# A state space layer computed in chunks of four tokens, inside a two-block network on one core

## The chip, the cores and the metric

The kernel runs on one core of one Trainium2 chip. The metric is device time in microseconds (us). TensorE (PE) multiplies matrices, VectorE (DVE), ScalarE (ACT) and GpSimd (POOL) do the rest, and DMA queues are fed by SyncE (SP) and by ScalarE's own instruction stream.

## The reference, cut to what matters

Two transformer blocks over 256 tokens of width 2048, all in float32. The part that changes is the state space layer ("SSM") of the second block: 64 groups of 16 channels, each with 64 complex states, so 32 tiles of 128 states for 8 tiles of 128 channels.

```python
    abar_re = mag * jnp.cos(li * dt)
    abar_im = mag * jnp.sin(li * dt)
    ...
    bu_re = jnp.einsum('blgh,gph->lbgp', ug, bbar_re)
    bu_im = jnp.einsum('blgh,gph->lbgp', ug, bbar_im)
    ...
    _, _, s_re, s_im = lax.associative_scan(_ssm_combine, (a_re, a_im, bu_re, bu_im), axis=0)
    y = (jnp.einsum('lbgp,ghp->blgh', s_re, c_re.astype(jnp.float32))
         - jnp.einsum('lbgp,ghp->blgh', s_im, c_im.astype(jnp.float32))
         + d_skip.astype(jnp.float32).reshape(SSM_GROUPS, SSM_GROUP) * ug)
    y = jax.nn.gelu(y.reshape(bsz, seq, SSM_WIDTH)).astype(u.dtype)
    return y * jax.nn.sigmoid(y @ w_glu + b_glu)
```

The matrices `abar`, `bbar` and `c` come from inputs, so they are worked out on the chip too.

## The kernel before

Six stages follow one another, named here as in the table below: pool, mlp0, attn, mlp1, mix2 (the SSM and the latent attention side by side), ffn. Activations lie transposed, features on the partitions and 256 tokens along the row. Weights stream once through the core: SP issues loads of 1 MB into three raw buffers; ACT makes the high part of each unit of 128x1024 numbers (`hi`, L145) and DVE the low part (`lo`, L153), three units ahead of PE (two for `lo` in mix2), with five buffers of each. PE then does the 16 to 24 matmuls of the unit (L203 to L211). That is one "tick" of some 2.8 us. After a tick the host code steps every live generator (the evacuation of a finished sum, in pieces) and runs one entry of a background list. So the program order of each engine, fixed when the kernel is built, is weight work with other work let in between.

The SSM appears in three places. `ssm_params` (pool stage, background, one step a tick) computes magnitudes, angles and the input and output matrices on DVE (L892 and others), turns them with 32 PE transposes (L948, L949) and writes them to DRAM (`d_q`). `tables` (mlp0, background, on POOL: L985, L991, L1005) doubles a table exp(i theta t) of every state up to 256 tokens and writes it to DRAM (`d_tab`, L1009). In mix2, `ssm_step` runs one of 32 tiles of states at a time: PE's `bu` (L1118, two float32 products, 256 columns, into PSUM), DVE's turn of `bu` by the table (L1063, 128x512, twice), POOL's two sums (`v`), DVE's two scans of 256 tokens (L1130), two turns back (`sp`, `sq`), and three tiles later PE's four `y` products (L1142, 256 columns). `ssm_pace` in the background list lets 1.2 to 1.4 half steps into each tick. The tables are loaded on ACT's queue (L1098, L1102). `gelu` finishes a tile of 128 channels (L1153 to L1161). The heads of the attention run as `scores`, `soft`, `flip` and `attend`; then the output slabs (`out`), the gate and its slabs.

Of the kernel before, what the change touches and what calls it, by code (L numbers as in the profile page):

```python
# [19 lines left out]
P = 128  # L20
T = 256
# [7 lines left out]
NS = 32  # L29
MAGIC = 1.5 * 2.0 ** 23  # L30
# [4 lines left out]
# how many units of weights are split ahead of the products (low parts: fewer where SBUF and VectorE are busy)  # L35
# [24 lines left out]
class Net:  # L60
# [12 lines left out]
    # ------------------------------------------------------------------ pools  # L73
# [39 lines left out]
    def want_slab(self, w, r0, nk, c0, nn=4):  # L113
        """nn tiles of columns: four, in loads of 4 k-tiles, or two, in loads of 8."""
# [42 lines left out]
    def take(self):  # L157
        """High parts are made ahead of low parts, and both ahead of the products, so that no engine waits."""
# [11 lines left out]
    # --------------------------------------------- work that follows a product, in steps  # L170
# [42 lines left out]
    def slab(self, nk, kx, on_done, n0=0, nn=4, raw=False):  # L213
        """nn tiles of columns of a product with the weights held: kx(k) is [P, 2T]."""
# [65 lines left out]
    def evac(self, acc, out, scale=None):  # L280
        """out = (main + correction) * scale"""
# [39 lines left out]
    def stats_sums(self, s, n, mean=False):  # L321
        """The sums over the partitions, then mean and deviation: [P tokens, half] in columns 0 and 8."""
# [22 lines left out]
    def spread(self, dst, m, col):  # L345
        """dst [P, T] <- a column for each half of the tokens, as a row on all partitions"""
# [3 lines left out]
    def rstd(self, s, n, name, box):  # L350
        """1 / the root mean square, in steps: box gets it as a row on all partitions, and as columns."""
# [44 lines left out]
    def norm_start(self, uses, sizes):  # L396
        """What the norm still has to do, before the work in the background; raw X is read `uses` times."""
# [68 lines left out]
    def raw_evac(self, acc, out, scale=1.0):  # L466
        """out = the product of the normed X (times scale), in steps"""
# [17 lines left out]
    def split_g(self, xs, src, g):  # L485
        """xs <- the parts of src * g"""
# [5 lines left out]
    # ------------------------------------------------------------------- setup  # L492
# [91 lines left out]
    # -------------------------------------------------------------- pool mixer  # L584
# [10 lines left out]
    def run_pool(self):  # L595
        nc = self.nc
        G = nc.gpsimd
        with ExitStack() as c:
# [7 lines left out]
            params = self.ssm_params(c.enter_context(self.tc.tile_pool(name="prm", bufs=1)))  # L606

            def more():
                if self.late:
                    self.late.pop(0)()  # L610
                if next(params, None) is not None or self.late:
# [55 lines left out]
    def residual(self, nk, kx, alpha, norm=None):  # L667
        """X <- alpha * X + product; a norm that follows is begun."""
# [24 lines left out]
    # --------------------------------------------------------------------- MLP  # L693
# [44 lines left out]
    # --------------------------------------------------------------- attention  # L738
# [122 lines left out]
    def cos_sin(self, x, cos, sin):  # L861
        """Of x within a turn; sin may be x."""
# [5 lines left out]

    def ssm_params(self, sp):
        nc, i = self.nc, self.i  # L870
        self.E1 = self.cst.tile([P, 2, NS], F32, name="E1")
        self.mag = self.cst.tile([P, NS], F32, name="mag")
        self.d_q = self.dram.tile([8, P, 640], F32, name="d_q")
        self.d_tab = self.dram.tile([NS, P, 512], F32, name="d_tab")
        nat = sp.tile([NS, 3, P], F32, name="nat")
        ldt = sp.tile([NS, 2, 1], F32, name="ldt")
        nc.sync.dma_start(out=nat[:, 0, :], in_=i["ssm_lambda_re_2"][0].rearrange("(s a) p -> s (a p)", a=2))
        nc.sync.dma_start(out=nat[:, 1, :], in_=i["ssm_lambda_im_2"][0].rearrange("(s a) p -> s (a p)", a=2))
        nc.sync.dma_start(out=ldt.rearrange("s a o -> s (a o)"), in_=i["ssm_log_dt_2"][0].rearrange("(s a) -> s a", a=2))
        nc.scalar.activation(ldt, ldt, AF.Exp)  # L880
        nc.vector.tensor_copy(nat[:, 2, :].rearrange("s (a p) -> s a p", a=2), ldt.to_broadcast([NS, 2, 64]))
        for _ in range(4):
            yield 1
# [4 lines left out]
        nc.vector.tensor_copy(pr, ps)  # L888
        lr, li, dt = (pr[:, n, :] for n in range(3))
        w = sp.tile([P, 12, NS], F32, name="wrk")  # L890
        th, k, nr, ni, den, zr, zi, t = (w[:, n, :] for n in range(8))
        tt = lambda o, a, b, op: nc.vector.tensor_tensor(out=o, in0=a, in1=b, op=op)  # L892
        cos, sin, mag = self.E1[:, 0, :], self.E1[:, 1, :], self.mag
        yield 1
# [4 lines left out]
        self.cos_sin(th, cos, sin)  # L899
        yield 1  # L900
        tt(nr, mag, cos, ALU.mult)
# [780 lines left out]
```

## Time and profile before

| what | us |
|---|---|
| median of 3 runs (3382.02 to 3385.28) | 3382.96 |
| span of the profiled execution | 3385.0 |
| PE busy in it | 3303.1 |
| DVE, ACT, POOL busy in it | 2276.1, 1591.9, 1228.8 |
| stages from: pool 0, mlp0 244, attn 994, mlp1 1472, mix2 2211, ffn 2641 | to 3385 |

The profiled execution's device time is its span; it lies 2.0 us above the median. The table is read so: PE is busy nearly all of the time, so what counts is PE's work and what PE waits for. In the rows further down a windows row is: from and to, length, then busy us and count of PE, PE's weight loads, DVE, ACT and POOL, the granted share of PE's clock, the DMA engines' share and GB/s. A timeline row is start, duration, engine, line, operation, tiles, count, and in brackets the idle time before it and what ended it. A waits row is who waited for what: us in all, times, longest. Float32 products show as two records each.

### The profile page before, as it was taken

Reading aid. Unit: us, or ns where it says so; the run is one execution under the profiler, and the core shown is the slowest. Engines: PE = TensorE matmul, PEld = TensorE weight load, DVE = VectorE, ACT = ScalarE, POOL = GpSimd, SP = SyncE. Lnnn points to the kernel's source line nnn. Section 1 sums busy time; section 2 is a strip of 40 time slices with the busy share of each in tenths; the row PEclk is TensorE's granted clock in tenths of the full one; section 3 lists DMA queues with packets and bytes.
Section 4 is the critical chain, followed back from the end, with each engine's and each line's share of the span. In section 5 each row is a group of like instructions: output and inputs, shape, how many; then the busy total and the mean of one; then the engine's idle time right before and its main releaser. Section 6 shows DMA issues by size and latency. Waiting matters only on the chain. (4 is left out here: it accounts for less than half of the span.)

```text
span 3385.0 us, 49181 instructions
## 1 busy us (share of the span) xinstructions
PE 3303.1 (98%) x19340; PEld 2873.5 (85%) x19340; DVE 2276.1 (67%) x2807; ACT 1591.9 (47%) x2428; POOL 1228.8 (36%) x1288
## 2 busy tenths in 40 slices
PE   8999999999999999999999999989999999999998
PEld 6888888888889989988888888887678888888887
DVE  6868576666675545586565656679796686687585
ACT  4555444444554444464444444563335544444344
POOL 5457666551350000072121211465566331132141
PEclk9999999999999999999999999999999999999999
DMA  7655666565554555445565556543335565555554
GB/s 209 214 175 178 203 213 211 195 221 188 176 193 153 172 175 174 150 152 193 178 199 186 181 182 198 178 139 117 103 116 162 162 194 192 174 187 199 185 179 171
DMA packets 421059, 603.18 MB, mean 178 GB/s; under 512 B 30052, under 2 KB 228570, under 8 KB 420826
## 3 DMA queue, kind: packets, MB, share of 16 engines
q1 hardware_dynamic: 414922, 588.43, 52.9%
q10 hardware_dynamic: 5760, 11.01, 1.1%
q8 instruction: 151, 2.47, 0.3%
q14 instruction: 82, 0.67, 0.1%
q0 software_dynamic: 144, 0.59, 0.1%
HBM read 586.87 MB, written 13.11 MB: 177 GB/s over the span
## 5 line engine op out<-in xcount | busy, mean ns | idle before, releaser
L153 DVE TENSOR_TENSOR lo<-raw,hi 128x1024 fp32r<-128x1024 f32 x1094 | 1470.9, 1370 | 541.2 <-ACT hi L145 540.2
L211 PE MATMUL acc<-xs,hi 128*128 128x512 f32 x4020 | 1429.7, 397 | 9.6 <-POOL xs L442 9.5
L145 ACT CAST hi<-raw 128x1024 fp32r<-128x1024 f32 x1094 | 1121.0, 1045 | 663.8 <-PE acc L211 465.7
L209 PE MATMUL acc<-xs,lo 128*128 128x256 f32 x4288 | 1165.2, 282 | 12.1 <-DVE lo L153 12.1
L211 PEld LDWEIGHTS acc<-xs,hi 128*128 128x128 f32 x4020 | 760.7, 189 | 177.0 <-POOL xs L442 11.4
L209 PEld LDWEIGHTS acc<-xs,lo 128*128 128x128 f32 x4288 | 813.8, 190 | 35.4 <-DVE lo L153 13.9
L211 PE MATMUL acc<-hid,hi 128*128 128x512 f32 x1920 | 683.3, 396 | 0.0
L209 PE MATMUL acc<-hid,lo 128*128 128x256 f32 x2048 | 555.7, 281 | 0.0
L684 POOL TENSOR_TENSOR X<-X,c 128x256 f32<-128x256 f32 x152 | 129.3, 862 | 898.9 <-DVE X L682 589.1
L211 PEld LDWEIGHTS acc<-hid,hi 128*128 128x128 f32 x1920 | 360.6, 188 | 81.3
L209 PEld LDWEIGHTS acc<-hid,lo 128*128 128x128 f32 x2048 | 384.6, 188 | 11.8
L298 POOL TENSOR_TENSOR hid<-t,hid 128x256 fp32r<-128x256 f32 x128 | 156.3, 1246 | 412.9 <-ACT hid L297 410.6
L288 ACT COPY c<-acc 128x256 f32<-128x256 f32 x264 | 98.0, 373 | 317.5 <-PE acc L211 307.9
L203 PE MATMUL acc<-xs,hi 128*128 128x256 f32 (+1 forms) x768 | 227.1, 296 | 15.4 <-ACT t L284 9.1
L204 PE MATMUL acc<-xs,hi 128*128 128x256 f32 (+1 forms) x768 | 222.9, 290 | 0.3 <-DVE xs L489 0.3
L205 PE MATMUL acc<-xs,lo 128*128 128x256 f32 (+1 forms) x768 | 221.8, 289 | 0.9 <-DVE lo L153 0.9
L1530 POOL TENSOR_TENSOR a<-t,r 128x256 f32<-128x256 f32 x88 | 67.0, 764 | 369.5 <-DVE t L289 347.0
L289 DVE TENSOR_TENSOR t<-acc,c 128x256 f32<-128x256 f32 x208 | 87.5, 422 | 164.1 <-ACT c L288 161.5
L203 PEld LDWEIGHTS acc<-xs,hi 128*128 128x128 f32 x768 | 151.4, 197 | 24.9 <-ACT t L284 10.0
L678 ACT COPY c<-acc 128x256 f32<-128x256 f32 x160 | 59.4, 373 | 204.2 <-PE acc L211 192.2
L205 PEld LDWEIGHTS acc<-xs,lo 128*128 128x128 f32 x768 | 151.9, 198 | 1.5 <-DVE lo L153 1.5
L204 PEld LDWEIGHTS acc<-xs,hi 128*128 128x128 f32 x768 | 152.1, 198 | 0.7 <-DVE xs L489 0.5
(304 smaller groups left out, 4421.0 us busy)
## 6 DMA issues: line engine op xcount, KB each, us to landing
raw<-in_mlp_w_up_dram SPq DMA_DIRECT2D x128, 1024.0 KB
raw<-in_mlp_w_down_dram SPq DMA_DIRECT2D x128, 1024.0 KB
raw<-in_ffn_w_up_dram SPq DMA_DIRECT2D x176, 512.0 KB
raw<-in_attn_w_qkv_dram SPq DMA_DIRECT2D x96, 512.0 KB
raw<-in_ffn_w_down_dram SPq DMA_DIRECT2D x44, 1024.0 KB
raw<-in_attn_w_qkv_dram SPq DMA_DIRECT2D x24, 1024.0 KB
raw<-in_pool_w_in_dram SPq DMA_DIRECT2D x16, 1024.0 KB
raw<-in_pool_w_out_dram SPq DMA_DIRECT2D x16, 1024.0 KB
```

What stands on the lines that cost most here:

```text
L145: self.nc.scalar.copy(to(hi), src)
L153: self.nc.vector.tensor_tensor(out=to(lo), in0=src, in1=to(hi).bitcast(F32), op=ALU.subtract)
L203: nc.tensor.matmul(acc[:, 0:n], lhsT=hi, rhs=x[:, 0:n], start=first, stop=False)
L204: nc.tensor.matmul(acc[:, 0:n], lhsT=hi, rhs=x[:, n:2 * n], start=False, stop=False)
L205: nc.tensor.matmul(acc[:, 0:n], lhsT=lo, rhs=x[:, 0:n], start=False, stop=last)
L209: nc.tensor.matmul(acc[:, T:2 * T], lhsT=lo, rhs=x[:, 0:T], start=False, stop=False)
L211: nc.tensor.matmul(acc, lhsT=hi, rhs=x, start=False, stop=last)
L288: nc.scalar.copy(c, acc[:, T:2 * T])
L289: nc.vector.tensor_tensor(out=out, in0=acc[:, 0:T], in1=c, op=ALU.add)
L298: (eng or nc.vector).tensor_tensor(out=xs[:, T:2 * T], in0=src, in1=xs[:, 0:T].bitcast(F32), op=ALU.subtract)
L684: (nc.vector if norm is not None and j >= KD - 2 else nc.gpsimd).tensor_tensor(out=x, in0=x, in1=c, op=ALU.add)
L1530: G.tensor_tensor(out=a[:, 2:], in0=t, in1=rs[0], op=ALU.mult)
```

## The change

Four tokens make a chunk (`CH` 4, `NJ` 64 chunks). States are kept at chunk ends only. The four tokens of a chunk and 32 channels fill 128 rows, so one input product takes 128 rows by 64 columns, and the output is a sum of three products (inputs of the same chunk, real and imaginary state before it). Each q (128 channels, 4 tiles of states) is one step, so there are 8 steps and not 32. Inputs are restacked from [channels, tokens] to [token in chunk and channel, chunk] by a write to DRAM (`d_u`) and four loads, and outputs back through `d_y`. `ssm_params` moves from the pool stage into mlp0's background list, computes powers up to the fourth of `abar` on DVE, shorter tables, and for each q the stacked matrices on POOL with PE transposes and products (`pd`), written to `d_b` and `d_c`. The rest of the diff (comments taken out, strided views for the new token order) is not shown.

```diff
-Q_BUFS, V_BUFS, S_BUFS, LAG = 1, 2, 2, 3
-PACE_IN, PACE_HEADS, PACE_OUT = 1.4, 1.2, 1.25
+W_BUFS, LAG = 5, 2
+PACE_IN, PACE_HEADS, PACE_OUT = 0.6, 0.6, 0.6
...
             if l == 0:
-                self.tables(c)
+                self.ssm_dram()
+                params = self.ssm_params(c.enter_context(self.tc.tile_pool(name="prm", bufs=1)))
...
+        cmul(e2, e1, e1)
+        cmul(e3, e2, e1)
+        cmul(ep[:, 0], e2, e2)
+        yield
+        for n in range(1, NK):
+            cmul(ep[:, n], ep[:, n - 1], ep[:, n - 1])
+            if n % 2 == 0:
+                yield
+        cmul(a2, a1, a1)
+        cmul(a3, a2, a1)
+        cmul(a4, a2, a2)
+        yield
...
+        for q in range(8):
...
+            for n in range(2):
+                pb = self.aux([P, 4, P])
+                for s in range(4):
+                    nc.tensor.transpose(pb[:, s, :], bm[n][:, s].rearrange("p l a h -> p (l a h)"), self.ident)
+                nc.scalar.copy(o[:, :, n, :], pb)
+                yield
+            nc.sync.dma_start(out=self.d_b[q], in_=o.rearrange("p s n c -> p (s n c)"))
...
+            pd = self.aux([P, P])
+            for n in range(2):
                 for s in range(4):
...
+                    nc.tensor.matmul(pd[32 * s:32 * s + 32, :], lhsT=bm[n][:, s, CH - 1].rearrange("p a h -> p (a h)"),
+                                     rhs=wl[n][:, s, 0:CH, :].rearrange("p l c -> p (l c)"), start=n == 0, stop=n == 1)
...
+            for l in range(CH):
+                r = slice(32 * l, 32 * l + 32)
+                if l:
+                    nc.sync.dma_start(out=self.d_c[q][r, :, 0, 0:32 * l], in_=zero[r, :, 0:32 * l])
+                for s in range(4):
+                    nc.sync.dma_start(out=self.d_c[q][r, s, 0, 32 * l:], in_=kt[32 * s:32 * s + 32, 0:P - 32 * l])
...
+            def load_u(q):
+                us[q] = sp.tile([P, 4, NJ], F32, tag="us", name="us", bufs=3)
+                for l in range(CH):
+                    load(out=us[q][32 * l:32 * l + 32], in_=self.d_u[q][:, l * NJ:(l + 1) * NJ].rearrange("(s f) j -> f s j", s=4))
...
+            def ssm_bu(q):
+                bus[q] = bu_p.tile([P, 2, T], F32, tag="bu", name="bu")
+                for s in range(4):
+                    m = qb[q, s // 2][:, s % 2]
+                    for n in range(2):
+                        nc.tensor.matmul(bus[q][:, n, s * NJ:(s + 1) * NJ], lhsT=m[:, n, :], rhs=us[q][:, s, :],
+                                         start=True, stop=True)
...
+                x = v.pop(q)
+                for s in range(4):
+                    for n in range(2):
+                        c = x[:, n, s * NJ:(s + 1) * NJ]
+                        V.tensor_tensor_scan(c, self.mag4[:, 4 * q + s:4 * q + s + 1].to_broadcast([P, NJ]), c, 0.0,
+                                             op0=ALU.mult, op1=ALU.add)
...
+            def ssm_out(q):
+                y = y_p.tile([P, 2 * T], F32, tag="y", name="y")[:, 0:T]
+                x = st.pop(q)
+                for s in range(4):
+                    c = slice(s * NJ, (s + 1) * NJ)
+                    m = qc[q, s // 2][:, s % 2]
+                    for n, r in enumerate((us[q][:, s, :], x[:, 0, c], x[:, 1, c])):
+                        nc.tensor.matmul(y[:, c], lhsT=m[:, n, :], rhs=r, start=n == 0, stop=n == 2)
...
+            def gelu(q, y):
+                yt = self.scr.tile([P, T], F32, tag="t", bufs=T_BUFS, name="yt")
+                nc.scalar.copy(yt, y)
+                load(out=self.d_y[q], in_=yt)
```

Where the change puts its work is seen in the program order of the engines. On DVE, the parameters stood in the pool stage; `wrk`, `prm` and `E` are small tiles of 128x32, `lo` is the weight work. Before:

```order
L153 TENSOR_TENSOR lo<-raw,hi 128x1024
L892 TENSOR_TENSOR wrk<-mag,E_315 128x32 x2
L903 TENSOR_SCALAR wrk<-wrk 128x32
L892 TENSOR_TENSOR wrk<-prm 128x32 x2
L892 TENSOR_TENSOR wrk<-wrk 128x32
L907 RECIPROCAL wrk<-wrk 128x32
```

After, on DVE in mlp0, the start of the second of seven steps of the parameters (`pw` are the powers):

```order
L156 TENSOR_TENSOR lo<-raw,hi 128x1024
L921 TENSOR_TENSOR pw_2967<-pw_2964,wrk 128x64
L921 TENSOR_TENSOR wrk<-wrk 128x32
L921 TENSOR_TENSOR mag_2296<-wrk 128x32
L941 TENSOR_SCALAR wrk<-pw_2967 128x32
L921 TENSOR_TENSOR wrk<-prm 128x32 x2
L921 TENSOR_TENSOR wrk<-wrk 128x32
L946 RECIPROCAL wrk<-wrk 128x32
```

Eight more follow ahead of the next `lo`. The whole chain left the pool stage; in mlp0 it is longer: 11, 16, 18, 12, 12, 24 and 26 small operations stand between eight successive `lo`.

On PE in mix2, one step of the SSM inside an output slab (`acc`) before:

```order
L205 MATMUL acc<-xs,lo 128x256
L1118 MATMUL bu<-u,qrec 128x256 x2
L1142 MATMUL y<-sp,qrec 32x256
L1142 MATMUL y<-sq,qrec 32x256 x2
L1142 MATMUL y<-sp,qrec 32x256
L203 MATMUL acc<-xs,hi 128x256
```

After, on PE, the third input step with the first output step, ahead of a latent slab:

```order
L207 MATMUL acc<-xs,hi 128x256
L208 MATMUL acc<-xs,lo 128x256
L351 MATMUL aux<-ident,m 128x128 x2
L1184 MATMUL bu<-us,qb 128x64 x8
L1219 MATMUL y<-us,qc 128x64
L1219 MATMUL y<-st,qc 128x64 x2
```

The last two rows come three times more. There are eight such places, the last `y` stands among the last heads, and the first output slab follows the last `attend` with no SSM product in it or after it.

On ACT in mix2, among the heads, before:

```order
L1357 COPY pt<-aux 128x384
L1102 DMA rec<-d_tab 128x512
L1342 ACTIVATE pr,sm<-pr,sm 128x256
L1342 ACTIVATE pr,sm<-pr,sm 128x128
L1102 DMA rec<-d_tab 128x512
```

After, on ACT, around the second output step (`half`: the rotary part's sums):

```order
L1166 DMA rec<-d_tab 128x512
L1157 DMA us<-d_u 32x4x64 x4
L148 CAST hi<-raw 128x1024
L287 COPY half<-acc 128x256 x2
L1162 DMA qb<-d_b 128x512 x2
L1227 COPY yt<-y 128x256
L1228 DMA d_y<-yt 128x256
L1171 DMA qc<-d_c 128x768 x2
```

ACT's stream in mix2 issues 120 DMAs where it issued 40, among the `hi` of the weights.

## Rows read from the trace of the kernel before

**Rows 1.** The page: busy time of the engines; the chain that ended last.
```profile
PE 3303.1 (98%) x19340; PEld 2873.5 (85%) x19340; DVE 2276.1 (67%) x2807; ACT 1591.9 (47%) x2428; POOL 1228.8 (36%) x1288
...
PE 22%; POOL 1%; DVE 1%; ACT 1%; issue 0%; ACTq 0%; POOLq 0%; DVEq 0%
```
**Rows 2.** Windows by stage (columns are told above): pool, mlp0, mix2.
```profile
0.00:244.00 244.00, 224.72 (x1270) 193.92 (x1271) 179.94 (x257) 123.09 (x205) 128.66 (x147) 0.99 0.63 200
244.00:994.00 750.00, 746.88 (x4363) 657.11 (x4362) 514.12 (x580) 363.96 (x528) 395.39 (x356) 1.00 0.60 198
...
2211.00:2641.00 430.00, 393.43 (x2560) 326.42 (x2559) 347.42 (x480) 193.67 (x378) 256.79 (x266) 0.94 0.40 124
```
**Rows 3.** Timeline of PE in mix2: one SSM step.
```profile
2495.76 0.28 PE L205 MATMUL acc<-xs,lo 128*128 128x256 f32 x1
2495.97 1.13 PE L1118 MATMUL bu<-u,qrec 32*128 32x256 f32 x4
...
2498.86 0.38 PE L203 MATMUL acc<-xs,hi 128*128 128x256 f32 x1
```
**Rows 4.** Timeline of PE at mix2's start: short float32 products.
```profile
2212.29 0.60 PE L331 MATMUL aux<-ones,Sq 128*128 128x1 f32 x4
2212.76 0.58 PE L331 MATMUL aux<-ones,X 128*128 128x1 f32 x4
```
**Rows 5.** What PE waited for in mix2.
```profile
PE acc L203 <- ACT t L284: 9.1, 4, 4.6
...
PE y L1142 <- DVE u L1153: 2.9, 2, 2.6
PE y L1142 <- DVE sp L1063: 2.2, 3, 1.1
...
PE bu L1118 <- POOL u L1063: 1.6, 1, 1.6
```
**Rows 6.** What ACT waited for in mix2.
```profile
ACT hi L145 <- DVE sq L1063: 59.0, 14, 6.9
```
**Rows 7.** Windows in mix2: last heads; a slab without SSM; last heads, L1142 alone.
```profile
2430.00:2470.00 40.00, 34.18 (x124) 19.40 (x124) 32.51 (x54) 11.61 (x32) 19.03 (x20) 0.80 0.21 56
2550.00:2570.00 20.00, 20.00 (x172) 20.00 (x172) 12.47 (x13) 15.68 (x32) 10.53 (x11) 1.00 0.56 174
...
2430.00:2470.00 40.00, 14.82 (x48) 5.26 (x48) 0.80 0.21 56
```
**Rows 8.** Timeline, DRAM: the issue of a write, and the first use after it.
```profile
533.24 1.79 SPq L1009 DMA_DIRECT2D d_tab<-w  x4
...
537.86 1.05 POOL L1005 COPY w<-w 128x128 f32<-128x128 f32 x1 [4.65 <-DMA d_tab<-w]
```
**Rows 9.** Windows in the pool stage: sixteen us with the parameters, sixteen behind them.
```profile
56.00:72.00 16.00, 10.30 (x45) 8.42 (x44) 14.78 (x27) 7.14 (x13) 11.06 (x16) 0.79 0.95 150
72.00:88.00 16.00, 15.35 (x90) 13.17 (x89) 15.29 (x19) 6.80 (x10) 15.10 (x16) 1.00 0.59 195
```
**Rows 10.** Timeline of PE there, and its transposes.
```profile
65.54 0.58 PE L209 MATMUL acc<-xs,lo 128*128 128x256 f32 x1 [3.95 <-DVE lo L153]
...
97.24 0.27 PE L948 MATMUL aux<-ident,bm 128*128 128x128 f32 x1
97.35 0.27 PE L949 MATMUL aux<-ident,cm 128*128 128x128 f32 x1
```
**Rows 11.** Timeline of DVE: small operations in the pool stage, then in mlp0.
```profile
58.37 0.72 DVE L892 TENSOR_TENSOR wrk<-mag,E 128x32 f32<-128x32 f32 x2
...
63.74 1.75 DVE L153 TENSOR_TENSOR lo<-raw,hi 128x1024 fp32r<-128x1024 f32 x1
...
286.20 0.69 DVE L969 TENSOR_TENSOR ept<-ep 128x64 f32<-128x64 f32 x1
286.93 0.19 DVE L970 TENSOR_TENSOR ep<-ept 128x32 f32<-128x32 f32 x1
...
289.55 1.22 DVE L153 TENSOR_TENSOR lo<-raw,hi 128x1024 fp32r<-128x1024 f32 x1
```

More of the change, by code (lines that the diff above doesn't have):

```diff
@@ L706, in run_mlp, with more @@
             if l == 0:
-                self.tables(c)
+                self.ssm_dram()
+                params = self.ssm_params(c.enter_context(self.tc.tile_pool(name="prm", bufs=1)))
+                def more():
+                    if next(params, self) is not self:
+                        self.bg.append(more)
+                self.bg.append(more)
             self.norm_start(2, NORM_TILES)
@@ L878, in ssm_params @@
-        nc.sync.dma_start(out=nat[:, 1, :], in_=i["ssm_lambda_im_2"][0].rearrange("(s a) p -> s (a p)", a=2))
-        nc.sync.dma_start(out=ldt.rearrange("s a o -> s (a o)"), in_=i["ssm_log_dt_2"][0].rearrange("(s a) -> s a", a=2))
+        bn = [sp.tile([P, NS, 16], F32, name=f"bn{n}") for n in range(2)]
+        cn = [sp.tile([P, 8, 64], F32, name=f"cn{n}") for n in range(2)]
+        msk = sp.tile([P, 4], F32, name="msk")
+        load(out=nat[:, 0, :], in_=i["ssm_lambda_re_2"][0].rearrange("(s a) p -> s (a p)", a=2))
@@ new lines, in ssm_params @@
+        load(out=nat[:, 1, :], in_=i["ssm_lambda_im_2"][0].rearrange("(s a) p -> s (a p)", a=2))
+        load(out=ldt.rearrange("s a o -> s (a o)"), in_=i["ssm_log_dt_2"][0].rearrange("(s a) -> s a", a=2))
+        load(out=msk, in_=i["c_mask"])
+        yield
+        for n, nm in enumerate(("ssm_b_re_2", "ssm_b_im_2")):
+            load(out=bn[n], in_=i[nm][0].rearrange("(s a) p h -> (a p) s h", a=2))
+        for n, nm in enumerate(("ssm_c_re_2", "ssm_c_im_2")):
+            load(out=cn[n], in_=i[nm][0].rearrange("(q s a) h p -> (s a h) q p", q=8, s=4))
@@ new lines, in ssm_params @@
+        for n, a in enumerate((a1, a2, a3, a4)):
+            V.tensor_copy(at[:, :, :, n], a)
+        yield
+        for b in range(4):
+            wt = sp.tile([P, 8, 2, NJ], F32, tag="w4", name="wt")
+            G.tensor_copy(wt[:, :, :, 0], e3[:, :, 8 * b:8 * b + 8].rearrange("p c s -> p s c"))
+            for n in range(NK):
+                m = 1 << n
+                tm = [sp.tile([P, 8 * 2 * NJ // 2], F32, tag=f"tmp{x}", name=f"tmp{x}") for x in range(2)]
+                tm = [x[:, 0:16 * m].rearrange("p (s c j) -> p s c j", s=8, c=2) for x in tm]
+                for x in range(2):
+                    e = ep[:, n, x, 8 * b:8 * b + 8].unsqueeze(2).unsqueeze(3).to_broadcast([P, 8, 2, m])
+                    G.tensor_tensor(out=tm[x], in0=wt[:, :, :, 0:m], in1=e, op=ALU.mult)
+                if n > 3:
+                    yield
+                for x in range(2):
+                    G.tensor_tensor(out=wt[:, :, x, m:2 * m], in0=tm[0][:, :, x, :], in1=tm[1][:, :, 1 - x, :],
+                                    op=ALU.subtract if x == 0 else ALU.add)
+                if n > 1:
+                    yield
+            for h in range(2):
+                for c in range(2):
+                    o = self.d_tab[2 * b + h].rearrange("p (c s j) -> p c s j", c=2, s=4)[:, c]
+                    nc.sync.dma_start(out=o, in_=wt[:, 4 * h:4 * h + 4, c, :])
+            yield
@@ L1106, in turn @@
                     tt(V, o, src, r[:, n:n + 1, :].to_broadcast([P, 2, T]), ALU.mult)
-            def pq(a, na, b, nb):
-                return (sp.tile([P, 2, T], F32, tag=t, name=t, bufs=n) for t, n in ((a, na), (b, nb)))
-            bus = {}
-            def ssm_bu(s):
-                q, sub = divmod(s, 4)
-                bus[s] = bu_p.tile([P, 2, T], F32, tag="bu", name="bu")
-                rows = slice(32 * sub, 32 * sub + 32)
-                for n in range(2):
-                    nc.tensor.matmul(bus[s][:, n, :], lhsT=qrec[q][rows, n * T:n * T + P], rhs=u[rows, q, :], start=True, stop=True)
@@ L1124, in ssm_in @@
+            def ssm_in(q):
+                p_, q_ = work("vp"), work("vq")
+                turn(p_, q_, bus.pop(q), rec[q])
+                v[q] = p_
                 tt(G, p_[:, 0, :], p_[:, 0, :], q_[:, 1, :], ALU.add)
                 tt(G, p_[:, 1, :], p_[:, 1, :], q_[:, 0, :], ALU.subtract)
-            def ssm_mid(s):
-                x = v.pop(s)
-                for n in range(2):
-                    V.tensor_tensor_scan(x[:, n, :], self.mag[:, s:s + 1].to_broadcast([P, T]), x[:, n, :], 0.0,
-                                         op0=ALU.mult, op1=ALU.add)
-                p_, q_ = st[s] = tuple(pq("sp", S_BUFS, "sq", S_BUFS))
-                turn(p_, q_, x, rec.pop(s))
@@ L1148, in run_mix2, with ssm_mid @@
[L1148 to L1154 removed]
+            def ssm_mid(q):
+                x = v.pop(q)
+                for s in range(4):
+                    for n in range(2):
+                        c = x[:, n, s * NJ:(s + 1) * NJ]
+                        V.tensor_tensor_scan(c, self.mag4[:, 4 * q + s:4 * q + s + 1].to_broadcast([P, NJ]), c, 0.0,
+                                             op0=ALU.mult, op1=ALU.add)
+                p_, q_ = work("sp"), work("sq")
+                turn(p_, q_, x, rec.pop(q))
+                st[q] = work("st")
+                to = st[q].rearrange("p n (s j) -> p n s j", s=4)
+                a, b = (t.rearrange("p n (s j) -> p n s j", s=4)[:, :, :, 0:NJ - 1] for t in (p_, q_))
+                G.memset(to[:, :, :, 0:1], 0.0)
+                tt(G, to[:, 0, :, 1:], a[:, 0], b[:, 1], ALU.subtract)
+                tt(G, to[:, 1, :, 1:], b[:, 0], a[:, 1], ALU.add)
@@ new lines, in run_mix2 @@
+            ys = []
+            def gelu(q, y):
+                yt = self.scr.tile([P, T], F32, tag="t", bufs=T_BUFS, name="yt")
+                nc.scalar.copy(yt, y)
+                load(out=self.d_y[q], in_=yt)
+                for _ in range(2):
+                    yield
+                uq = u[:, q, :]
+                for s in range(4):
+                    load(out=uq[32 * s:32 * s + 32].rearrange("p (l j) -> p l j", l=CH),
+                         in_=self.d_y[q][:, s * NJ:(s + 1) * NJ].rearrange("(l f) j -> f l j", l=CH))
+                for _ in range(2):
+                    yield
```

321 lines of the change are left out of this document (155 added, 166 removed).

## The prediction

> **What bounds the kernel now.** I began with the page's busy times and its chain [rows 1]: PE is at work for 3303.1 of 3385.0 us and leads the chain, so a change pays only where it takes work from PE or a wait that PE sits out. The windows by stage [rows 2] then show where that can be: mlp0 has 3 us of slack on PE in 750, so whatever is put on PE there is paid in full, and mix2 has 37 us of waits in 430 and a granted clock of 0.94. The timeline of one SSM step [rows 3] and the waits of the stage [rows 5, 6] show what the SSM costs there; two windows [rows 7] show the two kinds of stretch that mix2 has, one that PE's stream fills (172 matmuls in 20 us) and one that the heads' chain of engines fills (124 in 40 us, clock 0.80). The pool stage is read last, for what the parameters cost it [rows 9 to 11].
>
> **The change, part by part.** The sum is made against the span, 3385.0.
>
> *Pool stage, removed.* The parameters leave. Sixteen us with them hold 45 matmuls, the next sixteen 90 [rows 9]: 8 us are lost, a wait of 3.95 for a low part that stood behind the small DVE operations, and the lower clock after it [rows 10]. 32 transposes at 0.11, from start to start [rows 10], are 3.5 us, and their own waits for DVE's tiles some 3 more by the slack of the stage, 19 us in all [rows 2]. Together -15.
>
> *mlp0, PE work added.* 80 transposes at 0.11 are 8.8 us. 64 `pd` products are 128 records; the short float32 products run at 0.47 from group to group of four records [rows 4], 0.12 each, so 15 us at most; 32 places where PE leaves the stream and comes back at some 0.1 (the step of rows 3 begins 0.2 after the last matmul that normally takes 0.12) are 3. I take 26, with nothing to hide it, since PE never rests there.
>
> The Trainium skill, "TensorE: Matmul & The Clock Gate", Part 3, says that products which write different groups of 32 output partitions can run side by side; the four of `pd` do so. No row of before has four such in a row, and by that rule the 15 would be about 4. The sum goes by the row.
>
> *mlp0, DVE.* 119 small operations on 128x32 or 128x64 stand in seven ticks with one `lo` each. Their price is 2.62 us for 14, 0.19 each, where POOL rests, and 5.37 for 15, 0.36 each, where the pool stage has POOL busy most of the time; a single one has 0.69 [rows 11]. POOL is busy for 53% of mlp0 [rows 2], so I take the middle, 0.28: 33 us. Seven `lo` at 1.3 (1.22 and 1.75 in rows 11) and some 4 us of evacuation beside them make 46. PE needs 2.8 a tick for seven ticks, 20, and has three units in hand, 8. The stall is 119 x price - 15: 18 us at 0.28, 8 at 0.19, 28 at 0.36, 67 at 0.69. Behind the waiting `lo` are DVE's other evacuations, but PE waits for the `lo` first. The parameters' loads move from SP to ACT's queue, one tick of it, and the 21 small writes per q go on SP in one tick, some 9 us at 0.45 (1.79 for four in rows 8); three raw buffers, six units, 17 us, cover them, and if that cover goes each q would cost a few us. I add nothing. mlp0 in all: +44.
>
> *mix2, PE work.* A step takes PE from 2495.76 to 2498.86 between two matmuls that else stand 0.12 apart [rows 3]: 3.0 us, and 32 of them 95. Now there are 8 x (8 + 12) = 160 products of 128 rows and 64 columns. No row has that size; the nearest from below are the one-column products, 0.12 a record [rows 4], so 320 records are 38; from above the 256-column ones, 1.13 for four records, 0.28, would make 90. A one-column product cannot be paying for columns, so the 0.12 is a price per weight load, and 64 columns are a quarter of 256: 0.07 of 0.28. I take 38, range 38 to 90. That is -57.
>
> *mix2, waits removed.* PE's waits for SSM tiles (2.9, 2.2, 1.6 and three smaller groups, 9 in all) and for `t` on ACT (9.1) [rows 5]. The second is ACT's: its stream stands 59 us behind DVE's `sq`, because a table load waits for its buffer [rows 6]. DVE loses 96 of 128 turns and three quarters of the scans' columns. 18 us, and of the clock that is not granted (0.06 of 430 [rows 2], 26 us at most) half, 12. That is -30.
>
> *mix2, waits added.* Four terms. First, inputs go through DRAM: four issues of 0.45, then 2.8 from the last of four issues to the first use [rows 8], 4.6 a trip; the order has the write at least one half step ahead of the loads for most q, so I let three of eight trips show: 14. What is queued behind the waiting load is the next `hi`, and PE waits for that. Second, the last heads: in their window PE does 124 matmuls in 40 us, 48 of them the `y` records of six steps [rows 7], so the SSM work is partly filling there. Six steps are 18 us; DVE, at 32.51 of 40, loses its SSM work too, which shortens the heads' own chain, so I take half as not gained: 9. Third, the first output slab now follows the heads at once and waits for their norm, with a lower clock behind it: 8. Fourth, eight table loads still stand before a DVE chain on ACT's queue, against 32 before, with 9.1 us of PE's time in `t` before [rows 5, 6]: 2 to 9, taken as 6. Sum +37. Bounds: 15, when trips, loads and the heads hide, and 60, when all eight trips show (+23).
>
> mix2 is -57 - 30 + 37 = -50. The whole: -15 + 44 - 50 = -21, so 3364 by the span. The span lies 2.0 above the median, so **3362**.
>
> **The rivals.**
>
> *A larger gain.* mix2's added waits at 15 (-22), the small DVE operations at 0.19 (-10), `pd` side by side (-11): 3319. For it: PE in mix2 has slack of weights (DMA share 0.40 [rows 2]) and DVE loses most of its load. Against it: each of the three has to go well.
>
> *Flat.* All DRAM trips show, on ACT's queue ahead of the `hi`: +23, 3385, within 0.2% of before (0.2%, 7 us, is about what a measurement of this kernel can tell from no change).
>
> *Slower.* One mechanism: in mlp0 the small DVE operations run at POOL's pace, as the single 0.69 does with POOL at work [rows 11]. From 0.47 each on, the stall (41) eats the gain; midway to 0.69, at 0.58, it is 54, 36 more than I took, and the time 3398. For it: after the change POOL in mlp0 still has the split of the hidden tiles, and the 0.36 was seen with whole pairs at 0.72. Against it: the fifteen together show 0.36 with POOL busy, and of the parameters' own POOL work little runs in those seven ticks.
>
> The Trainium skill, "SBUF — State Buffer", "SBUF: two separate sides", says that a VectorE operation with both inputs in SBUF and a GpSimd operation that reads SBUF take a shared port in turn, each for its whole length. The 0.69 beside the 0.19 of rows 11 agrees; by that rule the 119 operations would pay a POOL operation each whenever POOL is busy, which is this rival.
>
> *The change doesn't do what it says*: the 64-column products cost what 256 columns do, 90 against 38; 3362 + 52 = 3414.
>
> **How the numbers follow.** The forecast as worked out (3340 to 3376) 0.46; the larger gain 0.18; flat 0.13; slower 0.20; no smaller products 0.03. Faster by over 0.2% is the first two, 0.64; within it 0.13; slower 0.23. The range leaves out the lower half of the larger gain and the upper half of the slower cases, 3316 to 3400.
>
> **What would show it.** In the profile after: windows by stage with pool near 229, mlp0 near 794, mix2 near 380. In mlp0, PE's waits for `lo` of about 18 us, all within seven ticks; if they are over 40, the slower rival holds. Small operations on DVE there at 0.28. `bu` and `y` records of 64 columns at 0.12 from start to start; `pd` at 0.12, or a quarter of it. In mix2, DVE's busy share well down from 347 of 430, PE's waits near 50, and among them the first output slab and ACT's `hi` behind loads. The prediction is wrong if mix2 stays above 400 (trips through DRAM show, or the heads' chain was the bound all along) or if mlp0 ends above 820.

## The result and the profile after

The changed kernel takes 3410.05 us (median of 4 runs, 3404.18 to 3415.47) against 3384.12: a ratio of 1.0079, 95% interval 1.0064 to 1.0093. It is slower by 26 us where 22 us faster was forecast. Its profiled execution took 3404.18 us, the shortest of the four, with a span of 3402.4; so the two traces differ by 17.4 us, and some 9 us more of the median are in executions that no trace shows.

Both kernels make the same 1094 low parts on DVE in the same order, so the start of the same one in both traces tells how far the changed kernel is behind at that point. Worked out from these starts:

```
from, to (low part)             change in us     forecast
pool stage (to the 81st)           -14.7            -15
mlp0, first part (to the 111th)    +16.6            +18
mlp0, the rest (to the 271st)      +24.5            +26
attn, mlp1 (to the 761st)           -3.0              0
mix2 (to the 821st)                 -6.3            -50
ffn                                 +0.3              0
```

The stages of after, in windows cut at the same points (from and to, length, busy us and count of PE, its weight loads, DVE, ACT, POOL; PE's granted clock; DMA share; GB/s), are pool, mlp0 and mix2, to be held against [rows 2]:

```profile
0.00:229.00 229.00, 218.13 (x1232) 189.06 (x1233) 152.71 (x192) 120.29 (x200) 129.44 (x147) 1.00 0.59 197
229.00:1020.00 791.00, 769.08 (x4574) 671.42 (x4573) 516.78 (x688) 378.40 (x575) 436.11 (x463) 0.99 0.61 194
...
2234.00:2658.00 424.00, 354.88 (x2497) 338.32 (x2497) 237.83 (x376) 196.36 (x386) 221.08 (x243) 0.86 0.45 138
```

The pool stage lost 15 us and mlp0 gained 41, as forecast. In mix2 DVE's load fell from 347 to 238 us, as the change has it, and yet the stage is only 6 us shorter: the granted clock went from 0.94 to 0.86. What PE waited for in mix2 of after (who, for what: us in all, times, longest):

```profile
PE bu L1184 <- DMA us<-d_u: 20.4, 4, 8.1
PE acc L206 <- ACT t L287: 15.2, 4, 9.6
PE aux L334 <- POOL Sq L322: 11.0, 2, 6.8
PE y L1219 <- POOL st L1120: 8.8, 3, 6.8
```

The first is new: the restacked inputs. The second was 9.1 before [rows 5]. To see what the clock adds, I divided the same stretch of mix2 (758th to 836th low part) of each kernel into PE's idle gaps, the busy time at half clock, and the rest, so that length = idle + half of the busy time at half clock + work at full clock:

```
kernel     length   idle   busy at half clock   work at full clock
before      389.2   32.9         38.4                337.1
after       383.0   64.4         88.8                274.2
```

PE's work fell by 63 us. 32 of them came back as idle time and 25 as work done at half clock. Counted from start to start of its products, PE spent 34 us of the stretch at half clock in the short products of the SSM (8 before), 16 in the heads' (5) and 37 in those of the weights (25).

One more wait is longer than before, the third: POOL's sums of squares (`Sq`) held PE for 6.8 us at 2299 to 2306, where before it waited 1.6 for POOL's `u` and 1.5 for these sums. The sums stand behind POOL's products that put the inputs into the new token order, in after and (second line) in before:

```profile
2297.15 5.77 POOL L1120 TENSOR_TENSOR ut<-u,r 128x256 f32<-128x256 f32 x4
2274.45 3.15 POOL L1063 TENSOR_TENSOR u<-u,r 128x256 f32<-128x256 f32 x4
```

No run takes this wait away.

### The profile page after: what moved, and what is told of

Same layout as the page of the kernel before. It is cut to its first block, busy times and chain, and to the rows that moved or that the text cites. A ratio compares the mean times of both kernels' runs of the same rounds, so it can differ in the third digit from the quotient of the medians.

```text
span 3402.4 us, 49683 instructions
## 1 busy us (share of the span) xinstructions
PE 3277.6 (96%) x19452; PEld 2892.3 (85%) x19452; DVE 2142.9 (63%) x2748; ACT 1606.5 (47%) x2477; POOL 1233.2 (36%) x1371
## 4 chain that ended last, share of the span: by engine, by line
PE 80%; POOL 10%; DVE 4%; ACT 2%; issue 2%; DMA 1%; ACTq 1%; SPq 0%; POOLq 0%; DVEq 0%
PE acc L214 37%; PE acc L212 20%; PE acc L277 4%; PE acc L276 4%; PE acc L275 4%; PE acc L211 2%; PE acc L206 2%; PE acc L207 2%; PE acc L208 1%; DVE lo L156 1%; POOL w L629 1%; POOL X L441 1%; POOL tmp L988 1%; POOL hid L301 1%; PE y L1219 1%
## 5 line engine op out<-in xcount | busy, mean ns | idle before, releaser
L301 POOL TENSOR_TENSOR hid<-t,hid 128x256 fp32r<-128x256 f32 x128 | 147.1, 1173 | 447.6 <-ACT hid L300 445.1
```

## The experiments

Every ratio below is to runs of the kernel before that were taken beside that run. Three theories for mix2. Theory 1: the loop from one input product over DVE, the table load and the input load to the next input product is longer than the 9.4 us that the pace gives a step (2 half steps at 0.6 a tick of 2.8 us), so PE waits, and each wait drops the clock. Theory 2: ACT's stream, with 120 DMA issues and their waits ahead of the weights' high parts, is what costs. Theory 3: the short float32 products hold the clock low themselves.

ACT's timeline in after at the longest wait for inputs (start, duration; ACTq is a DMA issue) shows the order that theory 1 speaks of:

```profile
2332.40 0.33 ACTq L1166 DMA_DIRECT2D rec<-d_tab  x1
2332.77 1.89 ACTq L1157 DMA_DIRECT2D us<-d_u  x4
2334.76 1.04 ACT L148 CAST hi<-raw 128x1024 fp32r<-128x1024 f32 x1 [7.53 <-issue]
```

The table load waited for its buffer, the input loads stood behind it although their data had been in DRAM for some time, and a high part behind both. The longest wait of all, 9.6 for `t`, has the same load at its root: DVE was done with the buffer (`sq`) at 2365.1, and ACT copies `t` behind the next high part, at 2368.45:

```profile
2365.18 0.34 ACTq L1166 DMA_DIRECT2D rec<-d_tab  x1
2365.56 1.89 ACTq L1157 DMA_DIRECT2D us<-d_u  x4
2367.50 1.04 ACT L148 CAST hi<-raw 128x1024 fp32r<-128x1024 f32 x1 [11.40 <-DMA rec<-d_tab]
```

So theories 1 and 2 name two sides of one blocked stream. PE's timeline at the end of the wait for inputs, and at a step without a wait:

```profile
2339.90 3.65 PE L1184 MATMUL bu<-us,qb 128*128 128x64 f32 x16 [8.15 <-DMA us<-d_u]
2343.34 0.64 PE L1219 MATMUL y<-us,qc 128*128 128x64 f32 x2
2343.76 1.06 PE L1219 MATMUL y<-st,qc 128*128 128x64 f32 x4
...
2374.13 0.39 PE L1219 MATMUL y<-us,qc 128*128 128x64 f32 x2
2374.35 0.61 PE L1219 MATMUL y<-st,qc 128*128 128x64 f32 x4
```

From start to start two records take 0.22 us at full clock and 0.42 behind the wait.

**Inputs first (u_first).** The loads of step q+1 stand ahead of the table load, half a step earlier.

```diff
                     if 0 <= q - LAG < 8:
                         ssm_out(q - LAG)
+                    if q + 1 in u_in:
+                        load_u(q + 1)
...
+                    if q + 1 in u_in and q + 1 not in us:
+                        load_u(q + 1)
                     if q < 7:
                         load_rec(q + 1)
-                    if q + 1 in u_in:
-                        load_u(q + 1)
```

> Only change to the kernel after: the four loads of the restacked inputs of step q+1 leave on ACT's queue right after the PE products of step q, ahead of the table load (which waits for DVE), where they left half a step later behind that load. Theory 1 (the loop from the input product over DVE, the table load and the input load to the next input product is longer than the 9.4 us that the pace gives a step, so PE waits, and each wait drops the clock): PE's wait for the restacked inputs falls from 20 us to under 6, PE's half-clock time in mix2 from some 123 us to under 95, time 3385 to 3396. Theory 2 (what costs is ACT's stream: DMA issues and their waits stand ahead of the weights' high parts and the evacuations): the table load still blocks ACT, time 3403 to 3410. Theory 3 (the short float32 products themselves hold the clock low): the wait goes, the half-clock time stays above 110 us, time 3395 to 3403.

3389.37 us, ratio to before 1.0014 [1.0004, 1.0024] (in brackets the 95% interval): 21 us won by an order of issue. PE's waits in mix2:

```profile
PE acc L206 <- ACT t L287: 15.6, 5, 8.6
...
PE bu L1184 <- DMA us<-d_u: 10.4, 4, 6.8
```

The wait for the inputs halved (not under 6), that for ACT stayed, and the busy time at half clock fell from 89 to 59 us. The time is theory 1's, with the remark that the clock gave more (15 us) than the waits (5).

**A slower pace (pace35).**

```diff
-PACE_IN, PACE_HEADS, PACE_OUT = 0.6, 0.6, 0.6
+PACE_IN, PACE_HEADS, PACE_OUT = 0.35, 0.35, 0.35
```

> Only change to the kernel after: 0.35 half steps a tick where there were 0.6, so a step gets 16 us and not 9.4, and the last steps fall into the output slabs. Theory 1: the loop of some 14 us now fits, PE's wait for the restacked inputs falls under 5 us, half-clock time in mix2 to 60 to 80 us, time 3360 to 3378. Theory 2: as many DMA issues and waits on ACT, only spread out; PE's waits for ACT's evacuations fall by half, time 3385 to 3398. Theory 3: as many short products, half-clock time still above 110 us, time 3395 to 3405.

3394.31 us (1.0038 [1.0023, 1.0052]). The wait for inputs is down to one of 8.0 us (not under 5), busy time at half clock to 63 us; but other waits came up (t on ACT 19.7, heads' `o` on ACT 9.6), so idle time stayed at 64. The loop was too long for the pace, and behind it stands ACT's stream. The time lies in theory 2's range, but its sign, ACT's waits halved, did not come; theory 1 was right on the direction of its wait and too hopeful on the time.

**Parameters' loads on SP (par_sp).**

```diff
-        load = nc.scalar.dma_start
+        load = nc.sync.dma_start
         nat = sp.tile([NS, 3, P], F32, name="nat")
```

> Only change to the kernel after: the eight loads of the state space parameters in mlp0 are issued by SP and not by ACT. If ACT's 8 us of issue there are what PE waits for (6.5 us for the transposes of the parameters, 2.9 us for an evacuation), mlp0 loses 8 to 11 us: 3399 to 3403. If the small DVE operations are what costs in these ticks, or the weights' loads behind the eight on SP come late instead, it stays within 4 us: 3406 to 3412.

3403.23 us (1.0061 [1.0046, 1.0076]), 7 us less than after, at the upper end of the first expectation; the interval overlaps that of after (1.0064 to 1.0093), so the gain is not clear of noise. The two traces' mlp0 differ by less, 3 us: the wait for the parameters' transposes (6.5 us, below) is gone, but that for low parts is 7.1 us for 6.3 and one for `xs` on POOL 4.8 for 2.7.

**All DMA issues of mix2's state space on POOL (mix_pool).**

```diff
-            load = nc.scalar.dma_start
+            load = nc.gpsimd.dma_start
             lj = lambda x: x.rearrange("p (j l) -> p l j", l=CH)
```

> Only change to the kernel after: all DMAs of the state space in mix2 are issued from POOL's stream and none from ACT's. Theory 1: the input load still stands behind the table load that waits for DVE, now in POOL's stream, so PE's wait for the restacked inputs stays at 15 to 30 us, time 3400 to 3415. Theory 2: ACT has no issue and no wait left, PE's wait for evacuations (15 us) and the late high parts go, time 3380 to 3395. Theory 3: half-clock time above 110 us either way.

3427.71 us (1.0131 [1.0116, 1.0147]). The wait for t on ACT fell from 15 to 7 us, as theory 2 has it, but PE's waits say what it cost:

```profile
PE bu L1184 <- DMA us<-d_u: 34.2, 4, 11.8
...
PE bu L1184 <- issue: 7.4, 1, 7.4
```

Freeing ACT alone does not help; the loop does not care which engine issues, and POOL is a link of it.

**Inputs first, tables half a step later (u_rec),** so that ACT no longer blocks.

```diff
+                    if 0 < q < 8:
+                        load_rec(q)
...
-                    if q < 7:
-                        load_rec(q + 1)
```

> The kernel after with the input loads of step q+1 right behind the products of step q, and the table load of step q behind those instead of half a step earlier, so that ACT's stream no longer waits there for DVE to be done with a table two steps back. Theory 1 (late issue): as with the input loads alone, 3386 to 3392, since the inputs set the loop. Theory 2 (ACT's stream): PE's wait for the evacuation t (15.6 us with the inputs moved alone) falls under 6 us and half-clock time in mix2 from 81 to 60 us, time 3370 to 3380.

3405.77 us (1.0061 [1.0046, 1.0076]): neither theory. The wait for t fell, as theory 2 said, and the time rose by 16 over u_first. PE's waits:

```profile
PE y L1219 <- POOL st L1120: 23.5, 8, 6.8
PE aux L334 <- POOL Sq L322: 11.0, 2, 6.8
PE acc L206 <- ACT t L287: 8.7, 6, 3.5
PE bu L1184 <- DMA us<-d_u: 6.8, 3, 4.1
```

At 0.6 half steps a tick the loop has one more member, the states (table, two turns, scans, POOL's sums): whatever is moved earlier, the next of them is waited for.

**Work into the waits (fill).** Wide products that nothing needs go ahead of the input products of the three steps that waited.

```diff
+                n_fill = {2: 36, 5: 18, 6: 24}.get(q, 0)
+                for k in range(n_fill):
+                    nc.tensor.matmul(bus[q].rearrange("p n t -> p (n t)"), lhsT=xs[:, 0, 0:P], rhs=xs[:, 0, 0:2 * T],
+                                     start=True, stop=True)
                 for s in range(4):
```

> The kernel after with products that nothing waits for put ahead of the input products of steps 2, 5 and 6 (36, 18 and 24 of 128x512, 0.21 us each at full clock, 16 us in all), where PE waited 8.2, 4.1 and 5.4 us. They go into the tile that the input products then overwrite. Theory 1 (a wait drops the clock, and the products behind it then cost double): half-clock time in mix2 falls from 121 us to under 90, the fill lies inside the waits, and the time falls by 5 to 20, 3390 to 3405. Theory 3 (the short products hold the clock low by themselves): half-clock time stays above 110 and the time rises by the part of the fill that the waits don't hide, 3408 to 3420.

3388.42 us (1.0017 [1.0007, 1.0026]): 22 us less than after, with 78 products more and every dependency as it was. PE's timeline at step 2, to be held against 3.65 above:

```profile
2330.42 8.46 PE L1183 MATMUL bu<-xs 128*128 128x512 f32 x36
2338.74 1.97 PE L1188 MATMUL bu<-us,qb 128*128 128x64 f32 x16
```

The wait for the inputs fell from 20.4 to 3.0 us since the fill covered it, which by itself wins nothing: the fill is 18 us of work (0.23 a product in the first line). What was won is the clock: busy time at half clock 46 us for 89. This run shows what stands behind these waits: 17 us of them covered gave 21 us of clock back.

**The changes together (all60, all45).** all60 is u_rec with par_sp; all45 is that at 0.45 half steps a tick.

> u_rec (input loads early, table loads late) with the parameters' loads on SP too. If the three causes add up, it is u_rec less 5 to 8 us: 3365 to 3383. If SP's loads only win by chance of the place, it is the same as u_rec.

3403.37 us (1.0051 [1.0035, 1.0068]), as u_rec within the scatter: the 7 us of par_sp, themselves not clear of noise, don't show here.

> all60 with 0.45 half steps a tick and not 0.6. Theory 1: a step has 12.5 us and not 9.4, PE's waits for the restacked inputs and for the states go under 5 us, two or three steps go into the output slabs, 3355 to 3372. If the heads' own chain of engines is the bound of that stretch, the waits only change their names and it is within 5 us of all60.

3374.77 us (0.9971 [0.9958, 0.9984]): it beats the kernel before by 0.3%, the first that does, and lies just above the range of theory 1. With 12.5 us a step the loop fits for the inputs, for which PE no longer waits; for states it still waits 8.2 us (not under 5). Idle time in the stretch is 41 us, for 64 in after.

```profile
PE aux L334 <- POOL Sq L322: 11.8, 3, 6.8
PE y L1219 <- POOL st L1120: 8.2, 3, 5.7
PE acc L206 <- ACT t L287: 8.0, 5, 3.5
```

**Around that point (first45, all35, tail).** first45 has u_first's early tables, all35 the pace 0.35, tail 0.45, 0.3 and 0.9 in the three phases.

> all45 with the table loads back where the kernel after has them (half a step earlier). If a late table delays the states (PE's wait for them was 23 us with late tables at 0.6 half steps a tick, 11 with early ones), PE's wait for states falls under 5 and the time is 3362 to 3372. If the blocked ACT stream counts for more, PE's wait for t rises from 8 to 15 us and it is 3378 to 3390.

3380.18 us (0.9988 [0.9978, 0.9998]). The wait for t rose to 12.6 us as expected for the blocked stream, and that for states fell only to 6.2.

> all45 with 0.35 half steps a tick throughout. Compared with pace35, which had the same pace, inputs and parameters as in the kernel after (3394): if the ACT order and SP's parameter loads count beside the pace, 3365 to 3380; if the pace alone sets it, 3385 to 3395.

3382.94 us (0.9994 [0.9985, 1.0004]): 11 us less than pace35 (15 by the two ratios), so the order and SP count beside the pace.

> all45 with 0.45, 0.3 and 0.9 half steps a tick in the three phases: the last state space step goes from the heads into the output slabs, whose wide products keep the clock up and hide waits. If the heads' end at half clock is what is left to gain: half-clock time in mix2 from 91 to 60 us, time 3355 to 3370. If the steps in the output slabs make PE wait for states as before the change, 3375 to 3385.

3382.2 us (0.9995 [0.9986, 1.0005]): busy time at half clock 86 us, not less. PE waited 11.1 us for states, 8.3 of them in the two waits behind the last heads, so this is the second outcome.

**What brings the clock back (fill45, blocks, fill45b).** In all45 PE ran at half clock from 2442 to 2486 us, in most of which it was busy, with short products and the heads' only. Windows of that stretch, of the one before it and of the one after it:

```profile
2405.00:2440.00 35.00, 30.21 (x194) 26.40 (x194) 20.31 (x44) 13.00 (x38) 18.36 (x23) 0.90 0.52 166
2442.00:2472.00 30.00, 28.98 (x104) 23.78 (x103) 12.51 (x31) 12.24 (x34) 10.11 (x15) 0.50 0.34 108
...
2486.00:2506.00 20.00, 20.00 (x173) 20.00 (x173) 14.46 (x23) 12.28 (x19) 10.05 (x10) 1.00 0.52 163
```

fill45 puts sixteen wide products ahead of the last input product there:

```diff
+                for k in range(16 if q == 7 else 0):
+                    nc.tensor.matmul(bus[q].rearrange("p n t -> p (n t)"), lhsT=xs[:, 0, 0:P], rhs=xs[:, 0, 0:2 * T],
+                                     start=True, stop=True)
```

> all45 (inputs early, tables late, parameters on SP, 0.45 half steps a tick) with sixteen products of 128x512 that nothing waits for ahead of the last input product, which stands among the last heads: there PE ran at half clock for 44 us, 30 of them without a wait, with short float32 products and the heads' alone. The fill is 3.4 us at full clock, 6.8 at half. If only waits lower the clock and it comes back by itself, the half-clock time of that stretch stays and the time rises by 3 to 7, 3377 to 3382. If wide products bring it back where short ones don't, the stretch falls from 44 us to under 30 and the time is 3364 to 3376 in spite of the added work.

3373.9 us (0.9971 [0.996, 0.9982]), no more than all45 in spite of the added work, and 59 us busy at half clock for 75. The time fits the second expectation, but the trace doesn't bear it out: the clock rose at 2456.1, two us ahead of the fill at 2458.5, amid the heads' products. So I measured the short products by themselves. blocks issues them with no waits, 300 in mlp1 amid wide products and 200 behind the wait for the norm's sums in mix2 (two records each); nothing uses their result. Both operands are the identity matrix.

```diff
+    def block(self, n):
+        ps = self.aux([P, 64])
+        for _ in range(n):
+            self.nc.tensor.matmul(ps, lhsT=self.ident, rhs=self.ident[:, 0:64], start=True, stop=True)
```

> The kernel after with two blocks of short float32 products (128 rows, 64 columns, nothing waits for them and they wait for nothing; their result is not used): 300 in mlp1, amid wide products at full clock, 66 us at 0.22 each, and 200 at the start of mix2 right behind the wait of 6.8 us for the sums of the norm, 44 us, where the clock was low for 6.8 us before wide products brought it back. If only waits lower the clock and any products bring it back: the first block runs at full clock throughout, the second is at half clock for 7 to 14 us. If short products lower the clock by themselves: it falls within the first block. If they don't lower it but can't bring it back: the first block at full clock, the second at half clock to its end (88 us).

One profile (3547.14 us with the added work). Windows inside the two blocks:

```profile
1540.00:1606.00 66.00, 66.00 (x594) 66.00 (x593) 6.78 (x7) 4.63 (x7) 10.16 (x9) 1.00 0.13 45
2344.00:2428.00 84.00, 84.00 (x396) 84.00 (x395) 3.27 (x10) 0.61 (x1) 0.00 (x0) 0.50 0.03 7
```

The third outcome: PE is busy all through both. Begun at full clock (2.4 GHz) the short products keep it for 66 us, at 0.111 a record; begun at half clock (1.2 GHz), behind a wait of 4.2 us, they stay there for 84 us, at 0.212, and the clock rose amid the wide products that follow them. Theory 3 in its first form falls: these short products did not lower the clock. But they did not bring it back either. The Trainium skill, "TensorE: Matmul & The Clock Gate", Part 1, says that idleness throttles PE and that keeping it busy releases it; the trace agrees with the first half (the clock fell within that wait of 4.2 us) and, for these products, not with the second. Whether the identity's zeros play a part no run shows. The SSM's own products agree as far as they go: behind the longest wait for inputs in after, 8.5 us of them ran at half clock, and the clock rose at 2351.3, amid the weights' products that began at 2348.4.

fill45b covers the two waits for states that are left in all45 with ten and twenty-six wide products ahead of the output products of steps 4 and 7.

> all45 with wide products that nothing waits for ahead of the output products of steps 4 (ten of 128x512) and 7 (twenty-six), where PE waited 2.2 and 5.7 us for the states in all45: 7.6 us of fill against 7.9 of waits. If the 44 us at half clock there hang on these waits, half-clock time in mix2 falls from 91 to 50 to 60 us and the time to 3355 to 3368. If they hang on the short products, it stays at 80 to 90 us and the time at 3372 to 3380.

3374.56 us (0.9972 [0.9961, 0.9984]). Half-clock time in the stretch is 76 us, for 91; busy time at half clock 61 for 75, a gain of 7 us against 10 us of fill. The low clock among the last heads doesn't hang on these two waits alone; what starts it there is left open.

## Why the prediction was wrong, by its own steps

*Pool stage: right.* -14.7 for -15, and by the terms named: divided as mix2 above, 8.3 us less idle time, 3.8 less work and 2.6 less loss by the clock.

*mlp0: the sum right (+41 for +44), its parts not.* Each q's four `pd` products with different output partitions ran side by side: in the trace four records begin within 0.02 us, and the next four 0.11 later. PE's timeline, sixteen records in one go:

```profile
445.00 0.65 PE L1061 MATMUL aux<-wl,bm 128*32 128x128 f32 x16
445.57 0.38 PE L212 MATMUL acc<-xs,lo 128*128 128x256 f32 x1
```

0.57 us, 0.036 a record and not 0.12; `pd` in all is 5 us for the 15 of the sum. The Trainium skill, "TensorE: Matmul & The Clock Gate", Part 3, says that such products can run side by side, and the trace agrees with it. The row that I took for the sum was not the nearest; with 0.036 its PE work is 16 us for the 26. Divided as mix2 above, the measured +24.5 are 16.6 us of work, 6.5 of idle time (3.4 for low parts, 3.1 for POOL's matrices) and 1.4 lost by the clock.

The +16.6 at mlp0's start have the size of the stall in the sum and other causes: 12.3 us of idle time, 3.8 lost by the clock and 0.6 of work. The 119 small DVE operations took 24 us from start to start, 0.20 each, near the lower bound; by the sum's own formula that is a stall of 9, and PE's waits for low parts in these ticks are 2.9. Twelve of them in 2.09 us, 0.17 each:

```profile
300.45 0.29 DVE L921 TENSOR_TENSOR wrk<-ep 128x32 f32<-128x32 f32 x2
...
302.54 1.22 DVE L156 TENSOR_TENSOR lo<-raw,hi 128x1024 fp32r<-128x1024 f32 x1
```

So the slower rival, small operations at POOL's pace, did not happen, and that was luck: it was hardly put to the test. I had taken POOL to be as busy there as in the whole stage, 53%; it was busy for 8.52 of the 44 us from 276 to 320, and idle for 25.83 on end. Two operations that met its long products took 0.71 each (first line); the last 26, beside short ones, 0.21.

```profile
286.75 1.42 DVE L921 TENSOR_TENSOR wrk<-prm 128x32 f32<-128x32 f32 x2
313.95 1.43 POOL L301 TENSOR_TENSOR hid<-t,hid 128x256 fp32r<-128x256 f32 x2 [25.83 <-ACT hid L300]
```

What PE waited for there comes in part from an edit that I had costed at nothing: the parameters' loads on ACT. ACT's timeline, and the waits of PE in mlp0:

```profile
269.69 5.35 ACTq L903 DMA_DIRECT2D bn<-in_ssm_b_im_dram  x1
275.07 2.52 ACTq L905 DMA_DIRECT2D cn<-in_ssm_c_re_dram  x1
...
278.33 1.04 ACT L148 CAST hi<-raw 128x1024 fp32r<-128x1024 f32 x1 [8.04 <-issue]
```

```profile
PE aux L912 <- DVE nat L908: 6.5, 1, 6.5
PE acc L212 <- DVE lo L156: 6.3, 3, 2.9
PE acc L211 <- DVE t L292: 2.9, 1, 2.9
```

The cover that I named (three raw buffers) is SP's; ACT's high parts have no such cover against 8 us of issue. How much of the +16.6 it is, par_sp bounds: with these loads on SP 12.9 are left in that stretch of its trace, since other waits came up, so the issue on ACT accounts for some 4.

*mix2, PE work: right.* -63 for -57; the 64-column product is 0.22, two records at 0.11, as taken.

*mix2, waits and clock: this is the step that failed.* I took -30 for waits and clock that go and +37 for what comes, +7 in all; the traces have +57: idle time +32 and the loss at half clock +25, and mix2 stands at 424, over the 400 that I had named as the sign of being wrong. Four terms were wrong.

First, the clock, the largest: I let it gain 12 us by the waits that go, and counted a little for the one wait that comes. I had not asked what PE does after a wait. Before, a wait was mostly followed by wide products (256 columns); after the change the waits for inputs and states are followed by up to forty short records, which ran at double price until the clock rose behind them.

Second, the trips through DRAM, 14 us for a measured 20.4. I priced one by its own length, 4.6 us, and let three of eight show. The row behind that price is a write's, and at the longest wait the load alone took 7.1 us from its first issue (2332.77) to PE's product (2339.90). Above all the loads were issued late, behind a table load that waits for DVE, in a loop longer than the pace allows; four trips showed, with waits of up to 8.1 us, and moving one link (u_rec, mix_pool) only passed the waits on.

Third, the 18 us of waits that I took as removed did not go. PE waits 8.8 for the SSM's states, about what the SSM cost in waits before, and 15.2 for `t` on ACT, where I had 9.1 going and 6 coming: one table load that waited for DVE held ACT, and PE with it, for 9.6. With the table loads later (u_rec) the wait for `t` was 8.7, but that for states 23.5.

Fourth, POOL's products for the new token order stood in the sum at nothing, and the waits for the squares behind them grew by 5. On the other side the 8 us for the first output slab did not come: between the last heads and 2617 us PE waits nowhere for more than 0.4 us. What became of the 9 for the heads no run separates.

The lower bound of the added waits, 15, does not come out of its terms either: with trips and heads at nothing and the table loads at 2, 8 + 2 = 10 are left.

*The rivals.* The flat rival had the right waits (input trips exposed on ACT's queue ahead of the `hi`) and nearly their size, 23 us for 20; what it lacked is the clock behind them and the waits that stayed. That fill comes to 3388, near its 3385, is chance: fill still has the other waits and 18 us of useless work.

## What to carry to other kernels

Before shortening work on PE, look at what it does right behind each wait: a wait costs its own length and, where short products followed it here, the doubled length of these until the clock rose; filling three of these waits with useless wide products won 22 us. A step of a software pipeline needs the whole loop of its dependencies within its pace, issues on in-order queues included: put the load whose data is ready ahead of the one that waits for a buffer, and choose the pace after that. Loads can hold the stream of the engine that issues them for microseconds (here four in a row 8.9 us, 5.35 of them the second, after 0.40 for a first of the same shape), so look at what stands behind them in that stream.

## What the runs showed of the hardware that was not expected

- Short float32 products (128 rows, 64 columns, of the identity; one run, blocks) kept a full clock for 66 us and did not regain it from half clock in 84 us of unbroken work.
- Four float32 products of 128 rows with outputs on different groups of 32 partitions ran at 0.036 us a record, where products over all output partitions ran at 0.11.
